# The gate stage of a one-layer trunk: where the last product's weights are split, and how 1 / rms is computed

## The chip, the core and the metric

One core of one Trainium2 chip runs the whole program. TensorE (PE) multiplies matrices, VectorE (DVE) and ScalarE (ACT) work elementwise, GpSimd (POOL) does elementwise work and issues DMAs that add to what is in memory, and SyncE (SP) issues the other DMAs. The metric is the device time of one execution in microseconds (us), lower being better.

## The reference, cut to what matters

With `DEPTH = 1` the layer is the sliding-window attention mixer, followed by a gated embedding and a last norm. Sequence length 512, width 2048, embedding width 256, all in float32:

```python
hn = rmsnorm(x, norm_g[0])
y = swa_mixer(hn, swa_w_in[0], swa_w_out[0], swa_sinks[0], rel_bias)
x = x + y
emb = p[0] @ ple_proj[0]
g = jax.nn.sigmoid(rmsnorm(x, ple_norm[0]) @ ple_gate[0])
x = x + emb * g
return rmsnorm(x, final_g)
```

where `rmsnorm(x, g)` is `x * rsqrt(mean(x * x) + EPS) * g` over each row. The mixer projects `hn` to queries, keys, values and a gate, attends over a window of 128 keys, multiplies by the gate, and multiplies by `w_out`. The gate stage is what follows `x = x + y`; the change touches it alone.

## The kernel before

**Float32 out of three passes.** A float32 operand is split into a rounded high part (a cast on ACT) and the rest (a subtraction on DVE). One product is then three matmuls, high by high, high by low and low by high (`mm3`, L126 to L128, each of 128 x 128 by 128 x 512).

**The stages.** Projections with the attention woven in; the out stage (the product with `w_out`); the gate stage (the product with `ple_gate`, the embeddings, the sigmoid, the sum and the last norm). In the out stage and the gate stage each product is cut into two by two blocks and computed from seven block products after Strassen's manner. Six are computed in the order `(1, 7, 6, 5, 3, 4)`; the seventh (number 2) is itself made of seven smaller ones (`Small`), spread among the first units of the stage.

**A unit.** `unit(p, jj, ...)` is one half (`jj`, 0 or 1) of block product `p`. It walks over four pieces `m` of weights (tiles of 128 x 1024) and does 12 matmuls for each. `B.get` (class `Pieces`) hands out the pieces: it starts the DMAs of coming pieces into `braw` or `grown`, some three to six ahead, and splits pieces up to two ahead: `bhi` on ACT (L754), `blo` on DVE (L755), in buffers three deep. After each piece the unit calls a share of the list `later`, then `todo()`, then `between()`. For the gate stage, `todo` does one step of preparing the next product's left operand (`ple_forms.steps`: a DVE sum into `hT`, L855, a cast `fhg`, L867, and a subtraction `flg`, L868) and, where the dictionary `early` names the place `(p, jj, m)`, calls `split_last(k)`.

**The last product (4).** Its eight pieces are loaded and grown (added up by POOL's DMAs) early, and are split ahead of their use: `split_last(k)` casts piece `k` into `last` on ACT (L762) and subtracts into `low` on DVE (L763). It is called for `k` from 0 to 6 at the places in `early`, and for 7 after the loop. When the loop is over, four `block` calls compute product 4, two halves by two row blocks, the last of them in two column halves.

**Embeddings and gate.** After some units, `embed` multiplies `pT` with a piece of `ple_proj` (12 matmuls per piece for two row blocks) into PSUM banks `t` or `o`. `gated` then does, for one row block and quarter of columns: the sigmoid on ACT (L1213, scaled by `rstd2`, the 1 / rms of the row), a product with the embedding on DVE (L1215), the sum into `x1` (by POOL's DMA, L1217, or on DVE, L1219), and a square with row sums (L1222 on ACT, L1224 on DVE). The last norm scales rows by 1 / rms (`row`, L1240; L1433; at the very end L1460 to L1471) and stores them.

**1 / rms.** `rsqrt_mean` (L162 to L177) makes the mean on DVE (L170), a square root on ACT (L171), then a reciprocal and one Newton step in five DVE instructions (L173 to L177). It is used for `rstd1` at the program's begin, for `rstd2` in product 1 of the gate stage, and for `yn2` twice while product 4 runs. For the last row block alone a power of -0.5 on GpSimd is used (L1457). ACT evaluates functions from a loaded table, and the square root and the sigmoid are in different tables; where the function changes, an `ACT_TABLE_LOAD` stands in ACT's queue.

**What sets the order.** From the second unit pair of the gate stage on, all five engines run in the order in which the program text issues instructions (`manual_schedule`); PE and SP do so throughout. Each engine takes its queue in order, so an instruction that waits holds up all behind it.

Of the kernel before, what the change touches and what calls it, by code (L numbers as in the profile page):

```python
# [11 lines left out]
F32 = mybir.dt.float32  # L12
F32R = mybir.dt.float32r
AF = mybir.ActivationFunctionType
ALU = mybir.AluOpType
# [3 lines left out]
D = 2048  # L19
S = 512  # L20
P = 128
KC = D // P
NB = S // P
# [14 lines left out]
EPS = 1e-6  # L38
# [17 lines left out]
def trunk_kernel(ctx: ExitStack, tc: tile.TileContext, a: dict):  # L56
    nc = tc.nc

    def pool(name, bufs=1, **kw):
        return ctx.enter_context(tc.tile_pool(name=name, bufs=bufs, **kw))  # L60
# [3 lines left out]
    const = pool("const")  # L64
# [93 lines left out]
    def run(gen):  # L158
        for _ in gen:
            pass  # L160

    def rsqrt_mean(out, ssq, n, nm):  # L162

        w = out.shape[-1]
        of = nm if w == 1 else "r"
        ms, rt, y, t = (
            const.tile([P, 1 if w == 1 else NB], F32, tag=f"{v}_{of}", name=f"{v}_{nm}")[:, :w]
            for v in ("ms", "rt", "y", "t")
        )
        nc.vector.tensor_scalar(ms, ssq, 1.0 / n, EPS, op0=ALU.mult, op1=ALU.add)  # L170
        nc.scalar.activation(rt, ms, AF.Sqrt)  # L171
        yield
        nc.vector.reciprocal(y, rt)  # L173
        nc.vector.tensor_mul(t, y, y)
        nc.vector.tensor_mul(t, t, ms)
        nc.vector.tensor_scalar(t, t, -0.5, 1.5, op0=ALU.mult, op1=ALU.add)
        nc.vector.tensor_mul(out, y, t)  # L177
# [21 lines left out]
    for k in range(KC):  # L199
# [67 lines left out]
        f, e = k == 0, k == KC - 1  # L267
# [118 lines left out]
    for t in range(NB):  # L386
        nc.vector.tensor_scalar_mul(values[t], v_ps[t][:, :256], rstd1[:, t : t + 1])
        nc.vector.scalar_tensor_tensor(
            out=values[t], in0=v_ps[t][:, 256:], scalar=rstd1[:, t : t + 1], in1=values[t], op0=ALU.mult, op1=ALU.add
# [154 lines left out]
    def turn(i):  # L544


        d, g = divmod(i, UNITS)
        pr = T.pop(i)
        pt = bank(f"pt{i}", "t")[:, :256]
        for u in range(2):  # L550
            nc.tensor.transpose(pt[:, u * P : (u + 1) * P], pr[:, u, :], ident)  # L551

        r = operands.tile([P, 2, 256], F32R, tag="r", name=f"r{i}", bufs=2)
        rh, rl = (r[:, l].rearrange("p (h u q) -> p u h q", h=4, u=2) for l in range(2))
        src = pt.rearrange("p (u h q) -> p u h q", u=2, h=4)
        nc.scalar.copy(rh, src)  # L556
        if g == 0:
            nc.vector.tensor_sub(rh[HB:], src[HB:], rh[HB:].bitcast(F32))
        else:
            nc.vector.tensor_sub(rl, src, rh.bitcast(F32))  # L560
        yield
        own = None
        if g >= 2:
            own = operands.tile([P, 2, 256], F32R, tag="own", name=f"own{i}", bufs=2)
            rows = slice(0, P) if g % 2 else slice(0, HB)
            flat = lambda v: v[rows].rearrange("p l (u q) -> p (l u) q", q=HB)


            sign = -1 if g % 2 else 1
            nc.gpsimd.affine_select(  # L570
                out=flat(own), in_=flat(r).bitcast(F32), pattern=[[0, 8], [sign, HB]], compare_op=ALU.is_ge, fill=0.0,
                base=-HB - 1 if g % 2 else 0, channel_multiplier=-sign,
            )
        PT[i] = (r, own)
        yield
        if own is not None:
            here, there = slice(HB, P), slice(0, HB)
            if g % 2 == 0:
                here, there = there, here
            nc.scalar.copy(own[there, 0], own[here, 1].bitcast(F32))  # L580
# [139 lines left out]
    class Pieces:  # L720
# [37 lines left out]
        def split_last(self, k, hi, lo):  # L758

            i = len(self.specs) - 8 + k  # L760
            raw = self.base.pop(i)
            nc.scalar.copy(hi, raw)  # L762
            nc.vector.tensor_sub(lo, raw, hi.bitcast(F32))  # L763
            self.made[i] = tuple([t[:, :512], t[:, 512:]] for t in (hi, lo))
# [387 lines left out]
    for n, p in enumerate(ORDER_OUT):  # L1152
        nxt = out_forms.steps(ORDER_OUT[n + 1]) if n < 5 else iter(())
        for jj in range(2):
# [3 lines left out]
            def between(m, ps):  # L1158
                q = small_steps.get((p, jj, m))
                if q is not None:  # L1160
                    small_out.prepare(q)
                for q in SMALL["w_out"].get((p, jj), {}).get(m, ()):
                    small_out.product(q)

            def todo():
                step = next(calls)
                part = x_at.get((p, jj, step))
                if part is not None:
                    load_x(part, nc.sync)
                next(nxt, None)  # L1170
                if p == 4:

                    for _ in range({0: 1, 1: 2, 2: 2, 3: 2, 5: 1, 6: 2, 7: 2}.get(4 * jj + step, 0)):
                        turn(*turns.pop(0), "o")
                    if jj:
                        next(ple_first, None)
# [13 lines left out]
    assert not turns  # L1190


    rstd2 = const.tile([P, NB], F32, name="rstd2")
    ss2 = const.tile([P, NB], F32, tag="sums", name="ss2")
    pT = wpool.tile([P, WE], F32, tag="wraw", name="pT").rearrange("p (k t) -> p k t", k=2)
# [5 lines left out]
    def embed(t, w, tag, c=slice(0, 512)):  # L1201
        e_ps = bank(f"e{t}_{done[t]}", tag)
        for k in range(2):
            mm3(e_ps[:, c], pTh[:, k, blk(t)], pTl[:, k, blk(t)], w[0][k][:, c], w[1][k][:, c], k == 0, k == 1)
        return e_ps
# [68 lines left out]


    rooms4 = {}
    early = {(5, 0, 3): 0, (5, 1, 1): 1, (5, 1, 3): 2, (3, 0, 1): 3, (3, 0, 3): 4, (3, 1, 1): 5, (3, 1, 3): 6}

    def split_last(k):
        if k % 2 == 0:  # L1280
# [16 lines left out]
    for n, p in enumerate(ORDER_PLE[:-1]):  # L1297
        if n == 1:

            ctx.enter_context(  # L1300
                tc.manual_schedule(
                    engines={getattr(mybir.EngineType, v) for v in ("PE", "SP", "DVE", "Activation", "Pool")}
                )
            )
        nxt = ple_forms.steps(ORDER_PLE[n + 1])
        for jj in range(2):
            calls = iter(range(4))

            def todo():
                k = early.get((p, jj, next(calls)))  # L1310
                while small_due:
                    small_due.pop(0)()
                if turns:
                    turn(*turns.pop(0), "t")
                    if not turns:
                        nc.vector.tensor_reduce(ss2, ssq2, axis=AX.X, op=ALU.add)
                        run(rsqrt_mean(rstd2, ss2, D, "r2"))
                    return
                next(nxt, None)
                if p == 1:  # L1320
                    next(nxt, None)
                if k is not None:
                    split_last(k)

            def between(m, ps):
                if (p, m) == (7, 3):
                    gate(p, jj, ps, None)
                q = ple_steps.get((p, jj, m))
                if q is not None:
                    small_ple.prepare(q)  # L1330
                for q in SMALL["ple_gate"].get((p, jj), {}).get(m, ()):
                    small_ple.product(q)

            ps = unit(p, jj, at_ple, ple_forms, todo, between)
            last_two, held_e = (p, jj) == (3, 1), {}
            if not (p == 7 or last_two):
                later.insert(0, partial_of(gate_later, p, jj, ps, held_e))
            for (of, which), j in EMBEDS.get((p, jj), ()):
                e = {}
                w = B.get(at_ple["e", (of, which)])  # L1340
                for t in (2, 3) if of == 5 else (0, 1):
                    e[t] = embed(t, w, "to"[which])
                held_e.update(e)
                if of == 1:
                    later.insert(which ^ 1, partial_of(gate_later, "sum", which, None, dict(e)))
                    held_e.clear()
            if p == 5:
                while moved:
                    later.extend(moved.pop(0))
        run(nxt)  # L1350
# [4 lines left out]
    w = [B.get(at_ple["e", (4, jj)]) for jj in range(2)]  # L1355
    f = ple_forms.made[4]
# [37 lines left out]
    yn2 = const.tile([P, 3], F32, name="yn2")  # L1394
    ssum = const.tile([P, 3], F32, name="ssum")
    nc.vector.tensor_reduce(ssum[:, :2], ssq3[:, :2, :4], axis=AX.X, op=ALU.add)
    root = rsqrt_mean(yn2[:, :2], ssum[:, :2], D, "r3")
    next(root)
    g = block(0, 0, "s", "o")()
    run(root)  # L1400
# [19 lines left out]
    lower, upper = slice(0, 256), slice(256, 512)  # L1420
    lower_ps = opened_bank(1, 1, "p", lower)
    nc.vector.tensor_reduce(ssum[:, 2:], ssq3[:, 2, :4], axis=AX.X, op=ALU.add)
    root = rsqrt_mean(yn2[:, 2:], ssum[:, 2:], D, "r4")
    next(root)
    g = block(0, 1, "p", "o")()
    run(root)
# [8 lines left out]
    next(g)  # L1435
    run(g)

    base, yn, power = (const.tile([P, 1], F32, name=f"{v}_3") for v in ("base", "yn", "power"))
    nc.gpsimd.memset(power, -0.5)
    g = block(1, 1, "p", "t", lower, opened_ps=lower_ps)()  # L1440
    next(g)
    by_gain(3, 0)
# [11 lines left out]
    run(last)  # L1454

    nc.vector.tensor_add(base, ssq3[:, 3, n - 1 : n], base)
    nc.gpsimd.tensor_tensor(yn, base, power, op=ALU.pow)  # L1457

    def scaled(x):
        nc.vector.tensor_scalar_mul(x, x, yn)  # L1460
# [66 lines left out]
```

## Time and profile before

| | us |
|---|---|
| median of 3 runs | 794.03 |
| lowest and highest of them | 792.91, 794.84 |
| the profiled execution, its own time | 792.63 |
| span of its profile, first to last instruction | 790.9 |
| PE busy in it | 779.9 |

The profile is one execution. A row of its timeline has the start in us from the span's begin, the duration, the engine, the line of the kernel, the operation and its operands (written from read, by the program's names with the buffer numbers left out), and in square brackets how long the engine had stood idle and what ended that. A row with `x2` is two instructions merged. The granted TensorE clock is 1.0 until PE's last matmul.

### The profile page before, as it was taken

How to read it: one execution, taken by the hardware profiler on the slowest of the kernel's cores; microseconds unless marked ns; L12 is line 12 of the kernel's file. 1: busy time of each engine (PE TensorE's matmuls, PEld its weight loads, DVE VectorE, ACT ScalarE, POOL GpSimd, SP SyncE). 2: the span in 40 equal slices, each digit the busy share in tenths (PEclk: the TensorE clock that was granted, in tenths of full speed). 3: DMA queues.
4: the chain of work that ended last, by engine and by line, in shares of the span. 5: the costliest groups of instructions: out<-in, count | busy, mean ns of one | idle time of the engine just before them, and what ended most of it. 6: DMA issues, size and time to landing. Idle time of an engine off the chain costs nothing.

```text
span 790.9 us, 11117 instructions
## 1 busy us (share of the span) xinstructions
PE 779.9 (99%) x3726; PEld 651.2 (82%) x3726; DVE 608.3 (77%) x1051; ACT 513.1 (65%) x1073; POOL 135.9 (17%) x254
## 2 busy tenths in 40 slices
PE   9999999999999999999999999999999999999995
PEld 7888888888888888888888888888888888887785
DVE  4556697877878687877777899778869598878895
ACT  6752576666767586766666654456689676566864
POOL 0200423131223223122222200000000022201000
PEclk9999999999999999999999999999999999999998
DMA  9988999999999989999997598667863999979633
GB/s 331 306 225 277 200 271 304 285 283 260 282 274 268 259 238 313 253 286 260 279 272 190 144 362 322 211 212 233 273 240 110 336 270 251 249 228 238 208 108 106
DMA packets 47561, 198.07 MB, mean 250 GB/s; under 512 B 7104, under 2 KB 8128, under 8 KB 41744
## 3 DMA queue, kind: packets, MB, share of 16 engines
q1 hardware_dynamic: 38208, 150.91, 54.8%
q0 software_dynamic: 9296, 46.46, 30.1%
q8 instruction: 29, 0.48, 0.2%
q14 instruction: 28, 0.23, 0.1%
HBM read 189.16 MB, written 71.35 MB: 329 GB/s over the span
## 4 chain that ended last, share of the span: by engine, by line
PE 96%; DVE 1%; ACT 1%; issue 0%; DMA 0%; POOLq 0%; DVEq 0%; SPq 0%
PE gps L126 7%; PE gps L127 7%; PE gps L128 7%; PE qps L126 7%; PE qps L127 7%; PE qps L128 7%; PE o L128 6%; PE o L127 6%; PE o L126 6%; PE g L127 4%; PE g L128 4%; PE g L126 4%; PE s L485 2%; PE vps L290 2%; PE pt L551 2%; PE o L598 2%
## 5 line engine op out<-in xcount | busy, mean ns | idle before, releaser
L755 DVE TENSOR_TENSOR blo<-braw,bhi 128x1024 fp32r<-128x1024 f32 x108 | 131.2, 1221 | 32.7 <-ACT bhi L754 31.8
L754 ACT CAST bhi<-braw 128x1024 fp32r<-128x1024 f32 x108 | 113.3, 1051 | 57.0 <-PE o L128 21.4
L127 PE MATMUL gps<-xl,whi 128*128 128x512 f32 x256 | 99.9, 390 | 0.0
L126 PE MATMUL gps<-xh,whi 128*128 128x512 f32 x256 | 99.9, 390 | 0.0
L128 PE MATMUL gps<-xh,wlo 128*128 128x512 f32 x256 | 99.7, 390 | 0.0
L126 PE MATMUL qps<-xh,whi 128*128 128x512 f32 x224 | 87.7, 392 | 0.0
L128 PE MATMUL qps<-xh,wlo 128*128 128x512 f32 x224 | 87.4, 390 | 0.0
L127 PE MATMUL qps<-xl,whi 128*128 128x512 f32 x224 | 87.4, 390 | 0.0
L110 DVE TENSOR_TENSOR wlo<-wraw,whi 128x1024 fp32r<-128x1024 f32 x60 | 73.5, 1226 | 2.9 <-ACT whi L109 2.8
L126 PE MATMUL o<-bhi,fho 128*128 128x512 f32 x192 | 74.8, 390 | 0.0
L128 PE MATMUL o<-bhi,flo 128*128 128x512 f32 x192 | 74.8, 389 | 0.0
L127 PE MATMUL o<-blo,fho 128*128 128x512 f32 x192 | 74.7, 389 | 0.0
L570 POOL TENSOR_SCALAR_AFFINE_SELECT own<-r 64x512 fp32r<-64x512 f32 (+1 forms) x48 | 32.5, 677 | 244.4 <-DVE r L560 228.6
L556 ACT CAST r<-pt 128x256 fp32r<-128x256 f32 x64 | 23.7, 371 | 67.7 <-PE pt L551 67.3
L109 ACT CAST whi<-wraw 128x1024 fp32r<-128x1024 f32 x60 | 62.3, 1040 | 4.6 <-issue 4.1
L127 PE MATMUL g<-blo,fhg 128*128 128x512 f32 x160 | 62.5, 391 | 0.7 <-DVE blo L755 0.7
L126 PE MATMUL g<-bhi,fhg 128*128 128x512 f32 x160 | 62.7, 392 | 0.0
L128 PE MATMUL g<-bhi,flg 128*128 128x512 f32 x160 | 62.3, 390 | 0.0
L128 PEld LDWEIGHTS gps<-xh,wlo 128*128 128x128 f32 x256 | 48.1, 188 | 10.2
L126 PEld LDWEIGHTS gps<-xh,whi 128*128 128x128 f32 x256 | 48.1, 188 | 9.1
L529 ACT ACTIVATE t<-t,sm 128x129 f32<-128x129 f32 (+1 forms) x128 | 49.7, 390 | 8.8 <-DVE sm L525 7.3
L127 PEld LDWEIGHTS gps<-xl,whi 128*128 128x128 f32 x256 | 48.1, 188 | 8.9
(239 smaller groups left out, 1768.7 us busy)
## 6 DMA issues: line engine op xcount, KB each, us to landing
wraw<-in_w_gate_in SPq DMA_DIRECT2D x32, 512.0 KB, 7.9
w_out<-in_w_out POOLq DMA_DIRECT2D x32, 512.0 KB, 9.0
braw<-w_out SPq DMA_DIRECT2D x32, 512.0 KB, 4.8
wraw<-in_w_q SPq DMA_DIRECT2D x28, 512.0 KB, 6.7
braw<-in_w_out SPq DMA_DIRECT2D x22, 512.0 KB, 4.4
braw<-in_ple_gate SPq DMA_DIRECT2D x22, 512.0 KB, 4.5
xw<-in_first SPq DMA_DIRECT2D x14, 640.5 KB, 7.0
w_out<-in_w_out SPq DMA_DIRECT2D x16, 512.0 KB, 10.6
```

The costliest lines, as they stand in the source:

```text
L109: nc.scalar.copy(hi, raw)
L110: nc.vector.tensor_sub(lo, raw, hi.bitcast(F32))
L126: nc.tensor.matmul(ps, sh, mh, start=first, stop=False, skip_group_check=more)
L127: nc.tensor.matmul(ps, sh, ml, start=False, stop=False, skip_group_check=more)
L128: nc.tensor.matmul(ps, sl, mh, start=False, stop=last, skip_group_check=more)
L290: nc.tensor.matmul(v_ps[t], h[:, c], part_of(high_at, 256, 512), start=f, stop=e, skip_group_check=True)
L485: nc.tensor.matmul(s_ps[:, u, : 2 * n], st, of_keys[:, first * 2 * QB : (first * QB + n) * 2], start=True, stop=True)
L529: nc.scalar.activation(su, su, AF.Exp, bias=sm[:, u : u + 1], accum_out=sm[:, 2 + u : 3 + u])
L556: nc.scalar.copy(rh, src)
L570: nc.gpsimd.affine_select(out=flat(own), in_=flat(r).bitcast(F32), pattern=[[0, 8], [sign, HB]], compare_op=ALU.is_ge, fill=0.0, base=-HB ...
L754: nc.scalar.copy(hi, raw)
L755: nc.vector.tensor_sub(lo, raw, hi.bitcast(F32))
```

## The change

Three edits, all in the gate stage:

- The dictionary `early` places the splits of product 4's pieces anew. Piece 0 stays after the fourth piece of the unit (5, 0). Before, the pieces 1 and 2 were split in the unit (5, 1) and two each of 3 to 6 in the units (3, 0) and (3, 1). Now the pieces 1 and 2 are split in (3, 0) and 3 to 6 in (3, 1).
- `power_of_mean` takes the place of `rsqrt_mean` for `rstd2` and both halves of `yn2`: the mean on DVE, then a power of -0.5 on GpSimd, with a constant tile of exponents that is set at the program's begin. The last row block uses the same constant.
- After `rstd2`, a sigmoid of one column is issued whose result nobody reads, so that the sigmoid's table is loaded there.

```diff
+    power = const.tile([P, NB], F32, name="power")
+    nc.gpsimd.memset(power, -0.5)
+
+    def power_of_mean(out, ssq, nm):
+
+        w = out.shape[-1]
+        ms = const.tile([P, NB], F32, tag="ms_r", name=f"ms_{nm}")[:, :w]
+        nc.vector.tensor_scalar(ms, ssq, 1.0 / D, EPS, op0=ALU.mult, op1=ALU.add)
+        yield
+        nc.gpsimd.tensor_tensor(out, ms, power[:, :w], op=ALU.pow)
+
...
-    early = {(5, 0, 3): 0, (5, 1, 1): 1, (5, 1, 3): 2, (3, 0, 1): 3, (3, 0, 3): 4, (3, 1, 1): 5, (3, 1, 3): 6}
+    early = {(5, 0, 3): 0, (3, 0, 0): 1, (3, 0, 2): 2, (3, 1, 0): 3, (3, 1, 1): 4, (3, 1, 2): 5, (3, 1, 3): 6}
...
-                        run(rsqrt_mean(rstd2, ss2, D, "r2"))
+                        run(power_of_mean(rstd2, ss2, "r2"))
+                        nc.scalar.activation(ss2[:, :1], ss2[:, :1], AF.Sigmoid)
...
-    root = rsqrt_mean(yn2[:, :2], ssum[:, :2], D, "r3")
+    root = power_of_mean(yn2[:, :2], ssum[:, :2], "r3")
...
-    root = rsqrt_mean(yn2[:, 2:], ssum[:, 2:], D, "r4")
+    root = power_of_mean(yn2[:, 2:], ssum[:, 2:], "r4")
...
-    base, yn, power = (const.tile([P, 1], F32, name=f"{v}_3") for v in ("base", "yn", "power"))
-    nc.gpsimd.memset(power, -0.5)
+    base, yn = (const.tile([P, 1], F32, name=f"{v}_3") for v in ("base", "yn"))
...
-    nc.gpsimd.tensor_tensor(yn, base, power, op=ALU.pow)
+    nc.gpsimd.tensor_tensor(yn, base, power[:, :1], op=ALU.pow)
```

## The prediction

> **What bounds the kernel now.** I read the page's head first, then three stages of the end, then who makes TensorE (PE) wait, then single instructions at those places.
>
> ```profile
> span 790.9 us, 11117 instructions
> PE 779.9 (99%) x3726; PEld 651.2 (82%) x3726; DVE 608.3 (77%) x1051; ACT 513.1 (65%) x1073; POOL 135.9 (17%) x254
> ```
>
> PE is the bound, so only time in which PE stands still, or the tail after its last matmul, can be won. By stage (columns: stage, its length, then busy time of each engine):
>
> ```profile
> 614.00:700.00 86.00, 86.00 (x384) 70.95 (x383) 67.25 (x72) 53.75 (x66) 13.77 (x16) 1.00 1.01 278
> 700.00:752.00 52.00, 50.44 (x221) 40.71 (x220) 45.10 (x51) 39.67 (x57) 7.09 (x9) 1.00 0.75 210
> 752.00:791.00 39.00, 30.41 (x163) 26.23 (x161) 29.70 (x62) 21.04 (x38) 0.57 (x1) 0.93 0.32 108
> ```
>
> The products 1, 7 and 6 of the gate stage (to 700) leave no hole in PE. Products 5 and 3 (700 to 752) leave 52.00 - 50.44 = 1.56 us. The rest is the last product and the tail. The holes are three, by the waits of PE in the out and gate stages:
>
> ```profile
> PE g L127 <- DVE blo L755: 0.7, 1, 0.7
> PE e L127 <- DVE blo L755: 0.7, 1, 0.7
> PE e L126 <- ACT bhi L754: 0.2, 1, 0.2
> ```
>
> "Idle" understates them, because a matmul shows 0.39 us busy while its follower normally starts 0.22 us after it. Starts tell more (start, duration):
>
> ```profile
> 708.46 0.39 PE L128 MATMUL e<-bhi,pTl 128*128 128x512 f32 x1
> 709.04 0.47 PE L126 MATMUL e<-bhi,pTh 128*128 128x512 f32 x1 [0.20 <-ACT bhi L754]
> 709.35 0.40 PE L127 MATMUL e<-blo,pTh 128*128 128x512 f32 x1
> ...
> 711.64 0.39 PE L128 MATMUL e<-bhi,pTl 128*128 128x512 f32 x1
> 711.86 0.39 PE L126 MATMUL g<-bhi,fhg 128*128 128x512 f32 x1
> 712.95 0.50 PE L127 MATMUL g<-blo,fhg 128*128 128x512 f32 x1 [0.70 <-DVE blo L755]
> 713.29 0.39 PE L128 MATMUL g<-bhi,flg 128*128 128x512 f32 x1
> ...
> 737.34 0.39 PE L126 MATMUL e<-bhi,pTh 128*128 128x512 f32 x1
> 738.40 0.50 PE L127 MATMUL e<-blo,pTh 128*128 128x512 f32 x1 [0.67 <-DVE blo L755]
> 738.74 0.40 PE L128 MATMUL e<-bhi,pTl 128*128 128x512 f32 x1
> ```
>
> Undisturbed, eleven steps from 709.35 to 711.86 take 2.51, 0.228 each, my pace below. Hole A: 708.46 to 709.35 is 0.89 for two steps, 0.43 too much. Hole B: 711.86 to 713.29 is 1.43, 0.97 too much. Hole C: 737.34 to 738.74 is 1.40, 0.94 too much. Together 2.34 us: all that the edits before the last product can give.
>
> **Part 1, the sigmoid's table.** What feeds A and B on ScalarE (ACT):
>
> ```profile
> 702.94 1.28 ACT L1213 ACT_TABLE_LOAD   x1
> 704.24 1.34 ACT L1213 ACTIVATE s<-s,rstd 128x512 f32<-128x512 f32 x2
> 705.48 0.60 ACT L867 CAST fhg<-hT 128x512 fp32r<-128x512 f32 x1
> 705.99 1.05 ACT L754 CAST bhi<-braw 128x1024 fp32r<-128x1024 f32 x1
> 706.94 1.04 ACT L762 CAST last<-grown 128x1024 fp32r<-128x1024 f32 x1
> 707.89 2.05 ACT L754 CAST bhi<-braw 128x1024 fp32r<-128x1024 f32 x2
> ```
>
> and on VectorE (DVE):
>
> ```profile
> 706.12 0.69 DVE L868 TENSOR_TENSOR flg<-hT,fhg 128x512 fp32r<-128x512 f32 x1 [1.93 <-ACT fhg L867]
> 707.07 1.23 DVE L755 TENSOR_TENSOR blo<-braw,bhi 128x1024 fp32r<-128x1024 f32 x1 [0.26 <-ACT bhi L754]
> 708.21 1.28 DVE L1215 TENSOR_TENSOR s<-e,s 128x512 f32<-128x512 f32 x2
> 709.41 1.21 DVE L855 TENSOR_TENSOR hT<-hT,hT 128x1024 f32<-128x1024 f32 x1
> 710.54 1.22 DVE L763 TENSOR_TENSOR low<-grown,last 128x1024 fp32r<-128x1024 f32 x1
> 711.68 3.49 DVE L755 TENSOR_TENSOR blo<-braw,bhi 128x1024 fp32r<-128x1024 f32 x3
> ```
>
> DVE idles 1.93 for a cast that stands behind the table load, and from 706.12 it works almost without a pause to the first blo of 711.68, which ends at about 712.90 and releases PE at 712.95. The second embedding at 709.04 writes a PSUM bank that L1215 at 708.21 must first have read, so A hangs on the same chain, whatever engine the row names. In the changed kernel the load is gone from here (its order has one table load in the whole gate stage, where the square root's was), so ACT and with it all six DVE rows start 1.30 earlier (702.94 to 704.24). L1215 starts at 706.91, A vanishes. The blo that B waits for starts at 710.38 and ends at 711.60. PE without A starts the second embedding at 708.69, its product's first matmul twelve steps on, at 711.42, and needs that blo at 711.65. So B vanishes too, with about nothing to spare. Gain 0.43 + 0.97 = 1.40. The early load costs nothing: it replaces the square root's load of the same kind at the same place in the queue, behind the same DVE instruction.
>
> The Trainium skill (ScalarE: Activation LUTs, What ACT_TABLE_LOAD costs) adds to each switch a drain of 1.38 us to 2.66 in all. The trace shows no such drain at 702.94, where 1.30 lies between load and sigmoid. By the page ACT would be freed 1.36 more; the sum would stay, since A and B hold no more, and only B's lack of spare would be cured.
>
> **Part 2, the splits.** Eight pieces of the last product are each cast on ACT (L762) and subtracted on DVE (L763). No split is added, seven keep their place in the sequence 0 to 6, and each is emitted at the same step or later. I counted, in the DVE order built from both kernels, how many L763 stand ahead of each blo. Numbering the last units' pieces from 107 (the one that hole B waits for): 107: 1 before, 1 after. 112: 2 and 1. 113: 3 and 1. 115: 3 and 2. 116 (the embedding of hole C): 4 and 2. 117: 4 and 3. 118: 5 and 3. 120: 5 and 4. 121: 6 and 5. Then equal. No blo gets more ahead of it; what can be lost comes only from PE being earlier.
>
> ```profile
> 719.57 1.23 DVE L763 TENSOR_TENSOR low<-grown,last 128x1024 fp32r<-128x1024 f32 x1 [0.26 <-ACT last L762]
> ...
> 726.70 1.23 DVE L763 TENSOR_TENSOR low<-grown,last 128x1024 fp32r<-128x1024 f32 x1 [0.64 <-ACT last L762]
> ...
> 735.99 1.22 DVE L763 TENSOR_TENSOR low<-grown,last 128x1024 fp32r<-128x1024 f32 x1
> 737.13 1.22 DVE L755 TENSOR_TENSOR blo<-braw,bhi 128x1024 fp32r<-128x1024 f32 x1
> ...
> 738.86 1.22 DVE L755 TENSOR_TENSOR blo<-braw,bhi 128x1024 fp32r<-128x1024 f32 x1
> ```
>
> The rows of 719.57, 726.70 and 735.99 leave the way to hole C and one comes in. A split takes 1.14 of DVE (735.99 to 737.13) and 0.95 of ACT (706.94 to 707.89). C's blo ends at 738.35. With two splits fewer it ends 2.28 earlier, at 736.07, if nothing else holds it. PE, earlier by 1.40, needs it at 737.34 + 0.23 - 1.40 = 736.17. Walking ACT and DVE in the new order from 711 with these durations (ACT held back where a cast must wait for PE to leave its three-deep buffer) I get 735.65, so 0.1 to 0.5 to spare. C vanishes: 0.94.
>
> What is late next is piece 117, now with a split right ahead. Before, its blo ran from 738.86 to 740.08 and was needed at 738.74 + 10 x 0.228 + 0.23 = 741.2. After, PE needs it 2.34 earlier, at 738.9; the walk gives 738.5, 0.3 to spare, and 0.6 for 118 by the same walk. From 119 on there are 2 us or more. I bound a new hole there from below by 0, from above by one split, 1.14; I take 0. ACT's casts of the two splits that leave the second half of product 5 go nowhere else than to the second half of product 3, and the DMAs are not moved: SP issues the same pieces in the same order, each as its buffer comes free, which is not later than now. The accumulating DMAs on POOL's queue wait for the DVE rows of kind L1215, which only move forward.
>
> **Part 3, the powers.** Three times, a mean on DVE, a square root on ACT and five small DVE steps become the mean and one power on GpSimd (POOL). The constant exponent is set once at the program's start, on POOL, which nothing waits for there but the identity of much later transposes.
>
> ```profile
> 760.21 0.17 DVE L170 TENSOR_SCALAR ms_r<-ssum 128x2 f32<-128x2 f32 x1
> ...
> 762.07 0.16 DVE L177 TENSOR_TENSOR yn<-y_r,t_r 128x2 f32<-128x2 f32 x1
> ```
> ```profile
> 784.22 0.57 POOL L1457 TENSOR_TENSOR yn<-base,power 128x1 f32<-128x1 f32 x1 [47.20 <-DVE base L1456]
> ```
>
> The old way takes 762.23 - 760.38 = 1.85 from mean to result. The power for one column takes 0.57. For two and four columns the trace has none: at least 0.57, at most that per column, 1.14 and 2.28; I take 0.57 plus 0.2 of handing over. The first result is made in product 1, before 614, and needed by the sigmoids at 704.24. The other two, of two columns and one, are needed by rows on DVE in the last product, where PE shows no hole and waits for no such row; there ACT also loses four table loads, by the built order. Nothing queues behind the powers on POOL but the last power. I cost the part at 0. If the cover were gone and each power also stood behind a DVE instruction of 1.23 (707.07), it would be late by 1.23 + 1.14 + 0.2 - 1.85 = 0.72 and 1.23 + 0.57 + 0.2 - 1.85 = 0.15, together 0.9.
>
> Against it speaks the Trainium skill (SBUF — State Buffer, Who interferes with whom): a GpSimd instruction that reads SBUF and a DVE one with two SBUF inputs shut each other out, the later one wholly. By that a power could hold a DVE subtract or wait for one, the case just priced; behind the cover named the sum keeps 0. No run here shows the two together.
>
> **Part 4, the tail.**
>
> ```profile
> 782.52 0.42 DVE L1215 TENSOR_TENSOR s<-e,s 128x256 f32<-128x256 f32 x1 [0.66 <-PE e L128]
> ```
>
> It starts when PE's last embedding is done, with DVE waiting 0.66. Its instructions stay the same, so it moves with PE's end.
>
> **Sum.** 0.43 + 0.97 + 0.94 - 0 = 2.34. Profiled execution: 792.63 us (span 790.9) less 2.34 is 790.3. That execution lies 1.4 under the median of the runs, 794.03, so for the median I say 791.7, 0.30% less. The runs spread from 792.91 to 794.84, about 1 us either way.
>
> **The rivals.**
> *Part of the holes stays.* B has next to nothing to spare and C 0.1 to 0.5; a bank, a buffer or a cast a little later than I walked keeps B or C open. For it: two of the three closings rest on tenths. Against: what is missing shortens a hole, it doesn't restore it whole. If B or C stayed whole, the gain is 1.4: 792.6.
> *The splits crowd.* Six of them now stand in the two halves of product 3, four in the second half, between 117 and 121. If DVE enters it late, each stands whole in PE's way: 4 x 1.14 = 4.56, less 2.34, is 2.2 slower: 796.2. It starts when the blo of 117 is 0.3 later than walked, and outweighs the gain from some 2.6. For it: DVE is busy 45.10 of 52.00 there. Against: each blo has no more ahead of it than before, and PE takes 12 x 0.228 = 2.74 per piece, against 2.28 of DVE for blo and split.
> *The powers come late.* Held by DVE instructions and dearer by the column, they cost DVE's rows in the last product the 0.9 of part 3, and with them the tail: 792.6. For it: no row shows a power beside DVE work or of two columns. Against: DVE's 0.66 wait ahead of the tail, which must be used up first.
> *The table is loaded again* at the first sigmoid would undo part 1; the built order has no such load, so I give it nothing of its own.
>
> **How the numbers follow.** All three holes close: 0.68. Part stays: 0.16. Crowding: 0.10. Late powers: 0.06. From the noise of this kernel 0.2%, 1.6 us, is about what can be told from no change. The first case gives faster 0.63 and, by scatter of the medians, same 0.05; the second 0.04 and 0.12; crowding slower 0.08 and same 0.02 (small holes only); late powers 0.03 and same 0.03. Sums: faster 0.70, same 0.22, slower 0.08. The range runs from 790.2 (2.34 and 1.5 of scatter) to 793.8, which takes in the partial gain with 1.2 of scatter and leaves out the crowding; the likeliest case alone is 790.6 to 792.8.
>
> **What would show it.** PE's starts pass 700 to 752 with no step over 0.4 (A, B, C gone) and PE's end is 2.4 earlier against the span's start. ACT has no table load after 700. DVE's blo of the embedding after product 3's first half is done before PE asks; if a wait of PE on L755 for one of the next two pieces appears, the splits crowd. POOL's powers show 0.57 whatever the columns; a DVE row L1251 waiting for POOL shows otherwise. I am wrong if PE's end moves by less than 1.6, or if the distance from PE's end to the span's end changes.

## The result, and the profile after

| | before, us | changed, us |
|---|---|---|
| median of 14 runs | 793.12 | 791.36 |
| lowest and highest | 792.79, 794.84 | 790.50, 793.31 |
| the profiled execution, its own time | 792.63 | 791.86 |
| span of its profile | 790.9 | 790.1 |

The ratio is 0.9977 with a 95% interval of 0.9969 to 0.9985: a small gain, but clear of no change. By the medians it is 1.76 us, 0.22%, where 2.34 us had been forecast. The predicted 791.7 lies 0.3 from the measured median, but that is luck in part: it was counted from 794.03, the median of three runs, and over 14 runs the kernel before has 793.12. Counted from there, 2.34 us less would have been 790.8.

The page's head of the changed kernel and its three last stages (columns as before):

```profile
span 790.1 us, 11098 instructions
PE 780.4 (99%) x3726; PEld 652.1 (83%) x3726; DVE 605.9 (77%) x1036; ACT 505.8 (64%) x1066; POOL 138.4 (18%) x257
```
```profile
614.00:700.00 86.00, 86.00 (x384) 70.94 (x383) 66.02 (x70) 54.68 (x68) 13.87 (x16) 1.00 1.00 279
700.00:752.00 52.00, 51.58 (x228) 42.33 (x227) 46.30 (x54) 38.98 (x57) 7.01 (x8) 1.00 0.78 215
752.00:791.00 39.00, 29.68 (x160) 25.62 (x158) 28.38 (x52) 15.09 (x32) 1.82 (x3) 0.91 0.32 108
```

PE's idle time from 700 to 752 fell from 1.56 to 0.42 us. What PE waits for in the out and gate stages is one row instead of three, and its place is hole B:

```profile
PE g L127 <- DVE blo L755: 0.4, 1, 0.4
```
```profile
712.12 0.39 PE L128 MATMUL e<-bhi,pTl 128*128 128x512 f32 x1
712.34 0.39 PE L126 MATMUL g<-bhi,fhg 128*128 128x512 f32 x1
713.15 0.50 PE L127 MATMUL g<-blo,fhg 128*128 128x512 f32 x1 [0.42 <-DVE blo L755]
713.49 0.40 PE L128 MATMUL g<-bhi,flg 128*128 128x512 f32 x1
```

From 712.34 to 713.49 is 1.15, so B still holds 1.15 - 0.46 = 0.69 of its 0.97. A and C are gone. In this execution the three holes are worth 2.34 - 0.69 = 1.65 us. PE's last matmul and the span's end show less: the one starts at 781.40 instead of 782.14, 0.7 earlier, and the span is 0.8 shorter, because this execution had lost 0.94 us to the earlier one by 700 us, in rows where both kernels have the same instructions on PE. A part of it recurs in each profile of the changed kernel (see "The powers in the last product" below).

```profile
782.14 0.28 PE L128 MATMUL e<-bhi,pTl 128*128 128x256 f32 x1
```
```profile
781.40 0.28 PE L128 MATMUL e<-bhi,pTl 128*128 128x256 f32 x1
```

Why B was left is to be read on ACT. First the row of the kernel before that starts its chain, then rows of the changed one:

```profile
696.08 1.05 ACT L754 CAST bhi<-braw 128x1024 fp32r<-128x1024 f32 x1 [2.46 <-DMA braw<-ple_gate]
```
```profile
697.69 1.05 ACT L754 CAST bhi<-braw 128x1024 fp32r<-128x1024 f32 x1 [3.13 <-DMA braw<-ple_gate]
...
702.96 0.62 ACT L867 CAST fhg<-hT 128x512 fp32r<-128x512 f32 x1 [2.96 <-DVE hT L855]
...
704.44 1.33 ACT L1224 ACTIVATE s<-s,rstd 128x512 f32<-128x512 f32 x2
705.68 0.60 ACT L867 CAST fhg<-hT 128x512 fp32r<-128x512 f32 x1
```

The table load is gone: no other row stands between casts and sigmoid. But the chain begins at the cast of piece 103, four pieces ahead of hole B, and there ACT stands idle until the piece's DMA lands: 2.46 us before, 3.13 now. DVE waits for that cast (698.78 below), then works without a pause up to `hT` (701.72), for which ACT's cast at 702.96 waits. So of the 1.30 us that the load gave, 0.67 was taken back by a later landing. From there DVE passes the delay on almost without a pause:

```profile
698.78 1.23 DVE L755 TENSOR_TENSOR blo<-braw,bhi 128x1024 fp32r<-128x1024 f32 x1 [2.96 <-ACT bhi L754]
...
701.72 1.21 DVE L855 TENSOR_TENSOR hT<-hT,hT 128x1024 f32<-128x1024 f32 x1
...
706.31 0.69 DVE L868 TENSOR_TENSOR flg<-hT,fhg 128x512 fp32r<-128x512 f32 x1 [0.51 <-ACT fhg L867]
707.27 1.23 DVE L755 TENSOR_TENSOR blo<-braw,bhi 128x1024 fp32r<-128x1024 f32 x1 [0.26 <-ACT bhi L754]
708.41 1.28 DVE L1226 TENSOR_TENSOR s<-e,s 128x512 f32<-128x512 f32 x2
709.61 1.21 DVE L855 TENSOR_TENSOR hT<-hT,hT 128x1024 f32<-128x1024 f32 x1
710.74 1.22 DVE L763 TENSOR_TENSOR low<-grown,last 128x1024 fp32r<-128x1024 f32 x1
711.88 3.49 DVE L755 TENSOR_TENSOR blo<-braw,bhi 128x1024 fp32r<-128x1024 f32 x3
...
736.18 1.22 DVE L755 TENSOR_TENSOR blo<-braw,bhi 128x1024 fp32r<-128x1024 f32 x1
...
739.06 1.21 DVE L755 TENSOR_TENSOR blo<-braw,bhi 128x1024 fp32r<-128x1024 f32 x1
...
781.79 0.42 DVE L1226 TENSOR_TENSOR s<-e,s 128x256 f32<-128x256 f32 x1 [1.53 <-PE e L128]
```

The row of 736.18 is the subtraction of hole C. It ends at 737.40, and PE asks for it at 737.80. That of 739.06 is piece 117, the one that had a split put right ahead of it. It ends at 740.27, and PE asks for it at 740.53, as if nothing were there:

```profile
740.30 0.39 PE L126 MATMUL g<-bhi,fhg 128*128 128x512 f32 x1
740.53 0.39 PE L127 MATMUL g<-blo,fhg 128*128 128x512 f32 x1
```

In the tail's first row (781.79) DVE now waits 1.53 us for PE, where it waited 0.66. The powers on POOL:

```profile
610.83 1.42 POOL L1202 TENSOR_TENSOR rstd<-ms_r,power 128x4 f32<-128x4 f32 x1 [157.70 <-DVE ms_r L1200]
...
760.21 0.72 POOL L1202 TENSOR_TENSOR yn<-ms_r,power 128x2 f32<-128x2 f32 x1 [23.10 <-DVE ms_r L1200]
...
772.36 0.54 POOL L1202 TENSOR_TENSOR yn<-ms_r,power 128x1 f32<-128x1 f32 x1 [11.42 <-DVE ms_r L1200]
```

The first of them shows a power beside DVE work, which the prediction had no row for:

```profile
610.66 0.68 DVE L868 TENSOR_TENSOR flg<-hT,fhg 128x512 fp32r<-128x512 f32 x1
611.36 1.23 DVE L755 TENSOR_TENSOR blo<-braw,bhi 128x1024 fp32r<-128x1024 f32 x1
```

Both subtractions take what they take elsewhere (0.68 and 1.23), so DVE was not held. Whether the power was held for a part of its 1.42 us, these rows don't tell.

### The profile page after: what moved, and what is told of

It reads as the page before. It is cut to its first block, busy times and chain, and to the rows that moved or that the text cites. A ratio compares the mean times of both kernels' runs of the same rounds, so it can differ in the third digit from the quotient of the medians.

```text
span 790.1 us, 11098 instructions
## 1 busy us (share of the span) xinstructions
PE 780.4 (99%) x3726; PEld 652.1 (83%) x3726; DVE 605.9 (77%) x1036; ACT 505.8 (64%) x1066; POOL 138.4 (18%) x257
## 4 chain that ended last, share of the span: by engine, by line
PE 93%; DVE 3%; issue 2%; ACT 1%; POOL 0%; POOLq 0%; DVEq 0%; ACTq 0%
PE gps L126 7%; PE gps L127 7%; PE gps L128 7%; PE qps L126 7%; PE qps L127 7%; PE qps L128 7%; PE o L127 6%; PE o L126 6%; PE o L128 6%; PE g L127 4%; PE g L128 4%; PE g L126 4%; PE s L485 2%; PE vps L290 2%; PE pt L551 2%
## 5 line engine op out<-in xcount | busy, mean ns | idle before, releaser
L126 PE MATMUL gps<-xh,whi 128*128 128x512 f32 x256 | 100.0, 391 | 0.0
L127 PE MATMUL gps<-xl,whi 128*128 128x512 f32 x256 | 100.0, 390 | 0.0
L126 PE MATMUL qps<-xh,whi 128*128 128x512 f32 x224 | 87.8, 392 | 0.0
L127 PE MATMUL qps<-xl,whi 128*128 128x512 f32 x224 | 87.4, 390 | 0.0
L127 PE MATMUL o<-blo,fho 128*128 128x512 f32 x192 | 74.9, 390 | 0.0
L126 PE MATMUL o<-bhi,fho 128*128 128x512 f32 x192 | 74.9, 390 | 0.0
L127 PE MATMUL g<-blo,fhg 128*128 128x512 f32 x160 | 62.5, 391 | 0.4 <-DVE blo L755 0.4
L126 PE MATMUL g<-bhi,fhg 128*128 128x512 f32 x160 | 62.8, 392 | 0.0
L126 PEld LDWEIGHTS gps<-xh,whi 128*128 128x128 f32 x256 | 48.1, 188 | 9.2
L127 PEld LDWEIGHTS gps<-xl,whi 128*128 128x128 f32 x256 | 48.1, 188 | 8.8
```

Source lines behind the costliest of these rows:

```text
L126: nc.tensor.matmul(ps, sh, mh, start=first, stop=False, skip_group_check=more)
L127: nc.tensor.matmul(ps, sh, ml, start=False, stop=False, skip_group_check=more)
```

## The experiments

Each kernel was measured beside runs of the kernel before. The ratio is an estimate of its own with a 95% interval, not the quotient of the two medians. Beside the times stand the three holes of one profiled execution, worked out as in the prediction, and ACT's wait for piece 103 in it:

| kernel | median, us | before, us | ratio, 95% interval | A, B, C, us | wait, us |
|---|---|---|---|---|---|
| before | | | | 0.44, 0.97, 0.94 | 2.46 |
| changed | 791.36 | 793.12 | 0.9977 (0.9969 to 0.9985) | 0, 0.69, 0 | 3.13 |
| old_places | 792.06 | 793.02 | 0.9994 (0.9985 to 1.0003) | 0, 0.01, 0.92 | 2.41 |
| new_places_only | 791.85 | 793.02 | 0.9990 (0.9981 to 1.0000) | 0.04, 0.94, 0 | 2.06 |
| late_table | 792.81 | 793.02 | 0.9995 (0.9986 to 1.0004) | 0.25, 0.96, 0 | 2.28 |
| split0_later | 790.61 | 793.02 | 0.9973 (0.9964 to 0.9982) | 0, 0, 0 | 2.40 |
| after_again | 791.32 | 793.05 | 0.9981 (0.9972 to 0.9990) | 0, 0.12, 0 | 2.57 |
| split0_again | 790.40 | 793.05 | 0.9967 (0.9954 to 0.9979) | 0, 0, 0 | 3.38 |
| roots_late | 790.18 | 793.05 | 0.9967 (0.9954 to 0.9979) | 0, 0.85, 0 | 3.39 |
| two_ahead | 793.06 | 793.05 | 0.9998 (0.9989 to 1.0007) | 1.29, 0.98, 0 | 2.73 |
| after_third | 791.96 | 793.09 | 0.9985 (0.9976 to 0.9993) | 0, 0.84, 0 | 3.39 |
| roots_again | 790.87 | 793.09 | 0.9975 (0.9964 to 0.9985) | 0, 0, 0 | 2.31 |
| split0_roots | 790.82 | 793.09 | 0.9974 (0.9965 to 0.9983) | 0, 0, 0 | 2.45 |

### Each part alone

**old_places**: the changed kernel, with the splits where they were.

```diff
-    early = {(5, 0, 3): 0, (3, 0, 0): 1, (3, 0, 2): 2, (3, 1, 0): 3, (3, 1, 1): 4, (3, 1, 2): 5, (3, 1, 3): 6}
+    early = {(5, 0, 3): 0, (5, 1, 1): 1, (5, 1, 3): 2, (3, 0, 1): 3, (3, 0, 3): 4, (3, 1, 1): 5, (3, 1, 3): 6}
```

> The changed kernel with the splits at their old places: only the powers and the early table load are left of the change. Theory (the time is PE's holes A, B and C ahead of the last product): A closes (0.43), B is left at about the 0.7 that the changed kernel shows, C stays open, because its four splits still stand ahead of piece 116; the gain is 0.4 to 1.1 us. Rival (the gain is made by fewer table loads and DVE steps in the last product and the tail): it stays whole, about 1.8 us, with C closed or not.

Its one wait of PE, and the start of B's chain on ACT:

```profile
PE e L127 <- DVE blo L755: 0.7, 1, 0.7
```
```profile
696.13 1.05 ACT L754 CAST bhi<-braw 128x1024 fp32r<-128x1024 f32 x1 [2.41 <-DMA braw<-ple_gate]
```

The row names `e`: it is hole C, 0.92, as in the kernel before. A and B are both shut. The gain, 0.96 us by the medians, is inside what the theory gave. The interval runs from a gain of 1.2 us to a loss of 0.2: it leaves out the rival's 1.8, but not that there is no gain, so it is the profile that tells which holes closed. B was expected to be left as in the changed kernel and was not: here the DMA landed as early as before, and the 1.30 of the table load was enough, with 0.01 of the hole left, as the prediction had walked it.

**new_places_only**: the kernel before, with the new `early` alone (the diff above, read backwards).

> The kernel before with the splits at their new places, nothing else. Theory: hole C closes, A and B stay as they were (0.43 and 0.97), the gain is about 0.9 us. Rival (last product and tail): no gain, since both table loads and square roots are still there.

```profile
PE g L127 <- DVE blo L755: 0.7, 1, 0.7
```

C is shut and B (`g`) stays at 0.94, as expected. The gain is 1.17 us by the medians against some 0.9, with an interval from 1.5 us down to nothing; the rival, no gain, falls by the closed hole rather than by the time. A was nearly shut too, with the shortest wait for piece 103 of all profiles, 2.06.

**late_table**: the changed kernel without the unread sigmoid.

```diff
-                        nc.scalar.activation(ss2[:, :1], ss2[:, :1], AF.Sigmoid)
```

> The changed kernel without the unread sigmoid: powers and new places stay, the sigmoid's table is loaded at the first sigmoid again, near 704 us. Theory: A and B come back to about 0.4 and 1 us or more, since 1.30 us of ACT is in their chain again; C stays closed; the gain falls from about 1.7 to 0.3 to 0.9 us. Rival (the powers make the gain): it keeps about 1.7 us and A and B stay as in the changed kernel.

```profile
702.93 1.28 ACT L1224 ACT_TABLE_LOAD   x1
704.22 1.34 ACT L1224 ACTIVATE s<-s,rstd 128x512 f32<-128x512 f32 x2
```

The load is back in the chain, A and B with it, and C stays shut. By the medians the gain is 0.21; by the profile's holes it is 2.34 - 1.21 = 1.1. The profiled execution was the fastest of its runs (791.64), and the interval holds both, and no gain as well. The profile says that the powers without the early load don't shut A and B.

### Hole B

**split0_later**: the changed kernel, with piece 0 split two places later.

```diff
-    early = {(5, 0, 3): 0, (3, 0, 0): 1, (3, 0, 2): 2, (3, 1, 0): 3, (3, 1, 1): 4, (3, 1, 2): 5, (3, 1, 3): 6}
+    early = {(5, 1, 1): 0, (3, 0, 0): 1, (3, 0, 2): 2, (3, 1, 0): 3, (3, 1, 1): 4, (3, 1, 2): 5, (3, 1, 3): 6}
```

> The changed kernel with piece 0 split in the unit (5, 1) after its second piece, past the subtraction that hole B waits for. Theory (B is the DVE queue between the embedding's landing and piece 107, in which the split takes 1.14): B closes, C stays closed, the gain is about 2.3 us against before, 0.7 more than the changed kernel. Rival (B is kept open by ACT, by the weights' DMA or by a buffer that PE frees late): B stays near 0.7 and the gain near 1.7 us.

On DVE the subtraction for piece 107 now follows `hT` at once, and PE's `L127` starts 0.23 after its `L126` like any other:

```profile
708.09 1.22 DVE L855 TENSOR_TENSOR hT<-hT,hT 128x1024 f32<-128x1024 f32 x1
709.22 2.35 DVE L755 TENSOR_TENSOR blo<-braw,bhi 128x1024 fp32r<-128x1024 f32 x2
```
```profile
711.55 0.39 PE L126 MATMUL g<-bhi,fhg 128*128 128x512 f32 x1
711.78 0.39 PE L127 MATMUL g<-blo,fhg 128*128 128x512 f32 x1
```

The first of the two ends near 710.4, 1.3 us before PE asks. All holes are shut and the gain is 2.41 us, where about 2.3 was expected. But this profile had an early landing, so **split0_again**, the same kernel, was run beside the changed one, **after_again**, and later the changed one once more, **after_third** (no edit in either).

> The kernel with piece 0 split past hole B's subtraction, beside the changed kernel on one chip. Theory: DVE has 1.14 us to spare at B, more than the 0.7 that a late DMA takes, so B is closed in each run, the median is 2.2 to 2.4 us under before and the runs scatter less than those of the changed kernel. Rival: equal to the changed kernel within 0.3 us.

> The changed kernel once more, for a second profile. Theory: the chain to hole B starts where ACT, idle, waits for the DMA of piece 103; in the first profile that wait ended 0.66 us later, against PE's place, than in the kernel before, and B kept 0.69. Where the wait is as short as in the profiles with 2.4 us of it, B is closed (under 0.2); where it is about 3.1, B is near 0.7. The median is about 1.8 us under before. Rival (B is kept open by the change itself, the same in each run): B near 0.7 whatever the wait.

> The changed kernel a third time, beside the two below on one chip. Theory: median about 1.8 us under before; the run's profile shows B at under 0.2 where ACT's wait for piece 103's DMA is 2.6 us or less, near 0.7 or more where it is above 3.

The casts of piece 103, first of after_again, then of after_third, then of split0_again:

```profile
696.78 1.05 ACT L754 CAST bhi<-braw 128x1024 fp32r<-128x1024 f32 x1 [2.57 <-DMA braw<-ple_gate]
```
```profile
697.86 2.12 ACT L754 CAST bhi<-braw 128x1024 fp32r<-128x1024 f32 x2 [3.39 <-DMA braw<-ple_gate]
```
```profile
697.17 2.13 ACT L754 CAST bhi<-braw 128x1024 fp32r<-128x1024 f32 x2 [3.38 <-DMA braw<-ple_gate]
```

The changed kernel's B goes with the wait: 0.12 at 2.57, 0.69 at 3.13, 0.84 at 3.39. With piece 0 out of the way, B is shut at 3.38 as well. The rival, a B that is the same in each run, has fallen. The five runs of split0_again lie between 790.13 and 790.79, the eleven of the changed kernel measured with it between 790.67 and 792.45; the medians are 0.92 apart, so the rival of equal times has fallen too. Split0_again gained 2.65 us where 2.2 to 2.4 was expected. The changed kernel gained 1.73 and then 1.13 us where about 1.8 was expected both times.

**two_ahead**: the changed kernel, with two splits ahead of B's subtraction instead of one.

```diff
-    early = {(5, 0, 3): 0, (3, 0, 0): 1, (3, 0, 2): 2, (3, 1, 0): 3, (3, 1, 1): 4, (3, 1, 2): 5, (3, 1, 3): 6}
+    early = {(5, 0, 2): 0, (5, 0, 3): 1, (3, 0, 2): 2, (3, 1, 0): 3, (3, 1, 1): 4, (3, 1, 2): 5, (3, 1, 3): 6}
```

> The changed kernel with two splits, 0 and 1, ahead of hole B's subtraction instead of one: a doubled cost. Theory: the holes A and B together hold 1.1 us more than in the changed kernel with the same wait for the DMA (1.1 to 1.8 us in all), C stays closed, and the gain on before falls to 0.5 to 1.2 us. Rival (a split ahead of B costs nothing, B is DMA or ACT alone): the time of the changed kernel.

```profile
PE e L126 <- DVE s L1226: 1.1, 1, 1.1
PE g L127 <- DVE blo L755: 0.7, 1, 0.7
```

A and B hold 2.27 together, where the theory had said 1.1 to 1.8, and no gain is left by the medians (793.06 against 793.05, where a gain of 0.5 to 1.2 had been expected; the interval reaches 0.9). The direction is the theory's: a split ahead of B is paid by PE. It is dearer than its 1.14 on DVE because DVE also stands idle for its cast:

```profile
707.63 1.23 DVE L763 TENSOR_TENSOR low<-grown,last 128x1024 fp32r<-128x1024 f32 x1 [1.12 <-ACT last L762]
```

In the changed kernel DVE waited 0.26 at this place, ahead of the subtraction at 707.27. The wait row for `e` also shows what can hold hole A: here PE waits for the DVE row that reads the PSUM bank (L1226, in the kernel before L1215). In the kernel before, that DVE row and the cast that the profile names end within 0.05 us of each other (708.89 and 708.94), and the trace can't tell which of them held PE.

### The powers in the last product

**roots_late** and, once more, **roots_again**: the changed kernel, with the two norms of the last product by square roots.

```diff
-    root = power_of_mean(yn2[:, :2], ssum[:, :2], "r3")
+    root = rsqrt_mean(yn2[:, :2], ssum[:, :2], D, "r3")
...
-    root = power_of_mean(yn2[:, 2:], ssum[:, 2:], "r4")
+    root = rsqrt_mean(yn2[:, 2:], ssum[:, 2:], D, "r4")
```

> The changed kernel with the two norms of the last product by square roots again (four table loads and ten DVE steps back); the power for the first norm, the early table and the new places stay. Theory: nothing in PE hangs on them, the time stays within 0.3 us of the changed kernel, and DVE's wait ahead of the tail's first row falls from 1.5 to about 0.6 us. Rival (the powers are what the change gains): it loses 1 us or more against the changed kernel.

> The kernel with square roots in the last product again, since its first time was 1.1 us under the changed kernel's in the same call, over only five runs. Theory: chance, from when the weights' DMAs land early in the program; it stays within 0.4 us of the changed kernel. Rival (square roots there are really quicker than powers): again 1 us under it.

The tail's first row in roots_late:

```profile
780.98 0.42 DVE L1226 TENSOR_TENSOR s<-e,s 128x256 f32<-128x256 f32 x1 [0.25 <-PE e L128]
```

It loses nothing: DVE is still ahead of PE, but by 0.25 instead of 1.53 us, where 0.6 had been expected. Both times the median came out 1.1 us under that of the changed kernel measured with it (790.18 to 791.32, 790.87 to 791.96), outside the expected 0.3 and 0.4, over five and eight runs. The end gives no place for that: from PE's last matmul to the span's end both kernels take 8.7 us, and the last product has no hole in either. B was 0.85 in one of the two profiles and shut in the other.

A part of it stands far ahead of the last product. From the matmul that starts at 95.08 in the profile of before to the one at 460.05 are 364.97 us. The other four profiles with square roots in the last product take 365.00 to 365.02 between the same two matmuls, the eight with powers there 365.33 to 365.41. PE shows no hole in between, only slightly longer steps, and up to 560 us PE, DVE and ACT have the same instructions in the same order in all thirteen. So the changed kernel loses 0.4 us there, and the two powers of the last product, late in the program, are what the eight have in common and the five lack. Why, and what makes the rest of the 1.1, is left open.

**split0_roots**: square roots in the last product, and piece 0 at its later place.

```diff
-    early = {(5, 0, 3): 0, (3, 0, 0): 1, (3, 0, 2): 2, (3, 1, 0): 3, (3, 1, 1): 4, (3, 1, 2): 5, (3, 1, 3): 6}
+    early = {(5, 1, 1): 0, (3, 0, 0): 1, (3, 0, 2): 2, (3, 1, 0): 3, (3, 1, 1): 4, (3, 1, 2): 5, (3, 1, 3): 6}
-    root = power_of_mean(yn2[:, :2], ssum[:, :2], "r3")
+    root = rsqrt_mean(yn2[:, :2], ssum[:, :2], D, "r3")
...
-    root = power_of_mean(yn2[:, 2:], ssum[:, 2:], "r4")
+    root = rsqrt_mean(yn2[:, 2:], ssum[:, 2:], D, "r4")
```

> Square roots in the last product and piece 0 split past hole B's subtraction. Theory: as the kernel with piece 0 moved alone, 2.2 to 2.6 us under before, no hole between 700 and 752. Rival (square roots are really quicker): 1 us less than that, 3.3 us under before.

The gain is 2.27, as the theory had it, and the rival's 3.3 is not met: with piece 0 at its later place, square roots gain nothing on powers (2.41 and 2.65). Its profile shows one reason. On ACT a piece of the second half of product 3 landed late, then the tail's first row on DVE, then PE's last matmul:

```profile
743.41 1.06 ACT L754 CAST bhi<-braw 128x1024 fp32r<-128x1024 f32 x1 [1.23 <-DMA braw<-in_ple_gate]
```
```profile
781.61 0.42 DVE L1226 TENSOR_TENSOR s<-e,s 128x256 f32<-128x256 f32 x1
```
```profile
780.45 0.28 PE L128 MATMUL e<-bhi,pTl 128*128 128x256 f32 x1
```

In the changed kernel that DVE row starts 0.39 after PE's last matmul (781.40 and 781.79); here it starts 1.16 after it, with no wait in its brackets: DVE itself is late, by 0.77, and the span grows by as much behind PE. With square roots DVE has 0.25 to spare at that place, and a landing that is late by about a microsecond uses it up. Two profiles with powers had the same landing late as well, after_third by 1.32 us and two_ahead by 1.73; there DVE still waited 1.19 and 1.53 us for PE at the tail's first row, and the tail kept its length.

## Why the prediction was right, and where its size was off

**The bound and the holes.** Right for the stretch it looked at: in the twelve profiles behind the first, the time between the same matmuls at 700 and 745 us follows the three holes within 0.1. It is not the whole account: ahead of 460 us the changed kernel loses the 0.4 us above, and the 1.1 us by which the kernel with late square roots was quicker is explained only in part. By its own sign the prediction would be wrong: PE's end was to move by at least 1.6, and against the span's start it moved by 0.73, 1.67 and 0.63 in the three profiles of the changed kernel, twice by too little; the profiled execution took 791.86 us where 790.3 was forecast. The sign left out that PE's place at 700 us differs from one execution to the next, in these profiles by 0.1 us earlier to 1.15 later than in the first.

**Part 1, the table.** Right in mechanism. old_places shuts A and B; late_table opens B whole again and A by 0.25. Where the DMA lands as in the profile of before, B closes with nothing to spare, as walked. The mis-sized term is B's 0.97: it was taken whole on the strength of one landing. The changed kernel closed 0.28, 0.85 and 0.13 of it in its three profiles. With what is left of B, the sums are 1.65, 2.22 and 1.50, and the medians measured with them moved by 1.76, 1.73 and 1.13; a profile is one execution and a median is not, so that the first pair lies so close is chance. The prediction walked the chain from the table load; it starts earlier, at a DMA for which ACT sits idle 2.1 to 3.4 us, and a margin of nothing there had to be laid beside that spread. "Part of the holes stays" named B first and for this reason (tenths), at 0.16, which was too little: B stayed open by 0.69 and 0.84 in two of three profiles.

**Part 2, the splits.** Right in both halves: C closes by the new places alone (new_places_only). In the first profile of the changed kernel its subtraction ends 0.40 ahead of PE, where 0.1 to 0.5 was walked, and piece 117 keeps 0.26 where 0.3 was walked. The crowding did not come in any profile.

**Part 3, the powers.** The cost of 0 held for what the prediction priced, the waits in the last product: late powers did not come, DVE's first scaled row there waited 0.25 us for POOL, and PE for nothing. The size did not hold: 0.57 was taken whatever the columns, and four took 1.42 and two 0.72, within the bounds given; the cover was wide enough. Two things were not in the account. The change itself uses up the cover of the tail: with the old square roots DVE would enter it with 0.25 instead of 1.53 to spare, and split0_roots shows one execution in which that costs 0.77. Against that stand the 0.4 us lost between 95 and 460 us in every profile with powers in the last product. Which of the two weighs more is not shown; by the medians the square roots were ahead by 1.1 us with piece 0 at its old place, and not ahead with piece 0 moved.

**The tail.** Right: 8.72 from PE's last matmul to the end, 8.80 before.

The version with all three edits and piece 0 at the later place (split0_later, split0_again) is the one in which each closed hole is accounted for: 790.61 and 790.40, 2.41 and 2.65 us under the kernel before. The kernel with late square roots and piece 0 at its old place (790.18 and 790.87, 2.87 and 2.22 us) can't be told from it by its times.

## What to carry to other kernels

A chain that ends in a stall is to be followed back until something waits for a DMA: a landing moves from run to run, and a walk that closes the stall with less to spare than the landing's spread closes it only some of the time. Work that may run at any time, like these splits, belongs behind the subtraction that PE is about to ask for, not only in fewer places ahead of it. Where PE is brought forward, look whether the engine that was comfortably ahead of it in the tail still is; here one execution shows what it costs when it is not. And before a change is put down to the place it edits, compare the same instructions far from that place: here 0.4 us went where no instruction had been edited.

## What the runs showed of the hardware

A power on GpSimd took 1.42 us for four columns, 0.72 for two and 0.54 for one in the changed kernel, and 1.42 or 1.43 for four in all eleven profiles that have it: neither flat nor in proportion. The rows can't tell the columns from being the first of its kind, or from waiting for DVE.

The wait for one DMA of 512 KB at the same place of the same instruction sequence lay between 2.06 and 3.39 us in thirteen profiles. What moves it was not tried.

PE's steps over the same instructions in the same order, with no hole, added up to 364.97 to 365.02 us in five profiles and to 365.33 to 365.41 in eight, by kernel and not by run. What in the kernels makes the difference was not tried.
